# A four-layer trunk on one core: first MLP block by token tiles, hi and lo planes regrouped, adaLN loads respread

## The chip, the core and the metric

The kernel runs on one core of a Trainium2 chip, as one program. The metric is device time in microseconds (us) of one execution. The engines named below are TensorE (PE in the rows, its weight loads PEld), VectorE (DVE), ScalarE (ACT), GpSimd (POOL) and SyncE (SP), whose instruction queue issues nearly all loads from memory.

## What is computed

256 tokens of width 1024 pass four layers. Each layer has a token mixer (MLA attention in layers 0 and 3, a gated convolution in layer 1, a pooling mixer in layer 2) and then an MLP. In outline, with `mod` the adaLN vector of the layer:

```python
c_act = silu(c)
for i in range(4):
    mod = c_act @ ada_w[i] + ada_b[i]           # 1024 x 6144
    sh_m, sc_m, gt_m, sh_f, sc_f, gt_f = split(mod, 6)
    h = rmsnorm(x, g[i, 0]) * (1 + sc_m) + sh_m
    y = mixer_i(h)
    x = x + gt_m * rmsnorm(y, g[i, 1])
    h = rmsnorm(x, g[i, 2]) * (1 + sc_f) + sh_f
    y = square(relu(h @ w1[i])) @ w2[i]         # 1024 -> 4096 -> 1024
    x = x + gt_f * rmsnorm(y, g[i, 3])
```

## The kernel before

Tokens lie in two tiles of 128. Every fp32 operand of the large products is split into a `hi` part of type fp32r and a `lo` rest, and a product is the sum of three matmuls: hi by hi, lo by hi, hi by lo. A weight tile of 512 KB arrives as `raw`; ScalarE casts it to `hi` (`load`, L173), VectorE subtracts to get `lo` (L174). There are 5 buffers for `raw` and 6 each for `hi` and `lo`.

**The MLP** (`ffn`) has 16 blocks of 256 hidden columns, c = 0 to 15. For a block, TensorE runs `colhalf` twice (L587, L589: the w1 part, into a bank h), ScalarE and VectorE make relu, square, and its parts gh and gl (L632 to L637), and TensorE runs `rowblock` (L561, L564, L565: the w2 part). The w2 part of a block is run behind the w1 part of the next, so that the relu chain lies beside it. The last two blocks share one `rowblock`, which goes through the four result banks y00, y01, y10, y11 one after the other.

**adaLN.** The product with `ada_w` is cut into units of 1 MB (`araw`, four buffers), eight units to a group (shift and scale of the mixer, of the MLP, or both gates). A unit is either multiplied on TensorE (`ada_mm`) or added up on VectorE (L222, `acc`, two instructions a unit); a group that has an `acc` ends with a flush on TensorE. The tables `MIX` and `FF` say how many units go into each block or stage, how many go to TensorE at the boundary, and how many loads are issued ahead at block 14 (`CF`): `ada_fetch(ahead)`.

**The boundary** between two stages (here: the head of a stage) is a chain. Squares of y, the gate row `bc_g`, the residual into xs, squares of xs, the scale `dg` (L371), transposes of tile 0 (L377), the same for tile 1 (L388, L395), and then the first block of the next stage. `bc_g` and `bc_a` are rows that GpSimd writes to memory (`rowd`) and reads back to all partitions.

**Order.** A list scheduler sets the order on PE, DVE, ACT and POOL; in heads `line()` fixes it in the order of the code. SP's queue has the order in which loads are written in the code. Each engine takes its instructions in its order, and an issue on SP waits until the buffer that it fills is free.

## Time and profile before

| what | value |
|---|---|
| median of three runs | 1191.03 us (1190.92 to 1191.21) |
| the profiled execution | 1190.78 us, span 1189.0 us |
| TensorE busy | 1137.4 us, 96% |
| VectorE busy | 848.2 us, 71% |
| ScalarE busy | 647.1 us, 54% |
| mean granted clock of TensorE | 0.982 of full speed |

The span is the time from the first to the last instruction on the core; the rest of the execution's 1190.78 us lies around it. Busy time counts matmuls, vector and scalar instructions, not waits and not the issue of transfers. A start in a timeline is counted from the beginning of the span.

### The profile page before, as it was taken

How to read it: one execution, taken by the hardware profiler on the slowest of the kernel's cores; microseconds unless marked ns; L12 is line 12 of the kernel's file. 1: busy time of each engine (PE TensorE's matmuls, PEld its weight loads, DVE VectorE, ACT ScalarE, POOL GpSimd, SP SyncE). 2: the span in 40 equal slices, each digit the busy share in tenths (PEclk: the TensorE clock that was granted, in tenths of full speed). 3: DMA queues.
4: the chain of work that ended last, by engine and by line, in shares of the span. 5: the costliest groups of instructions: out<-in, count | busy, mean ns of one | idle time of the engine just before them, and what ended most of it. 6: DMA issues, size and time to landing. Idle time of an engine off the chain costs nothing.

```text
span 1189.0 us, 17562 instructions
## 1 busy us (share of the span) xinstructions
PE 1137.4 (96%) x6654; PEld 917.5 (77%) x6654; DVE 848.2 (71%) x1205; ACT 647.1 (54%) x1144; POOL 52.9 (4%) x120
## 2 busy tenths in 40 slices
PE   7899989999999999999999989999998999999997
PEld 4667768888868867778788768787867877888886
DVE  3699688777665666868887777787776996655554
ACT  3364575556653244655565465455555665656553
POOL 1000010000010010000000210000011001000000
PEclk9999989999999999999999989999998999999999
DMA  9768758588726784878887567789625432765550
GB/s 347 300 276 314 298 220 316 220 317 298 267 72 240 257 312 188 312 308 353 327 321 279 201 233 280 304 337 337 243 80 214 164 115 81 234 199 187 182 190 36
DMA packets 73384, 290.01 MB, mean 244 GB/s; under 512 B 9986, under 2 KB 15234, under 8 KB 61012
## 3 DMA queue, kind: packets, MB, share of 16 engines
q1 hardware_dynamic: 70484, 280.44, 64.4%
q0 software_dynamic: 2816, 8.46, 2.0%
q8 instruction: 52, 0.85, 0.3%
q14 instruction: 32, 0.26, 0.1%
HBM read 286.57 MB, written 2.29 MB: 243 GB/s over the span
## 4 chain that ended last, share of the span: by engine, by line
PE 55%; DVE 5%; ACT 3%; DMA 3%; issue 3%; POOL 2%; SPq 0%; DVEq 0%; POOLq 0%; ACTq 0%
PE h L587 14%; PE y L561 7%; PE h L589 7%; PE y L564 7%; PE y L565 7%; PE dw_ps L986 2%; ACT junk L135 1%; DMA raw<-in_w_dram 1%; PE pw L561 1%; PE adap L256 1%; PE pw L565 1%; PE pw L564 1%; POOL r L121 1%; DVE acc L222 1%; DVE lo L174 1%
## 5 line engine op out<-in xcount | busy, mean ns | idle before, releaser
L174 DVE TENSOR_TENSOR lo<-raw,hi 128x1024 fp32r<-128x1024 f32 (+1 forms) x336 | 395.5, 1195 | 133.9 <-ACT hi L173 132.8
L173 ACT CAST hi<-raw 128x1024 fp32r<-128x1024 f32 (+1 forms) x336 | 339.8, 1029 | 98.6 <-PE h L587 37.6
L587 PE MATMUL h<-hT,hi 128*128 128x512 f32 x1024 | 367.1, 401 | 0.0
L589 PE MATMUL h<-hT,lo 128*128 128x256 f32 x1024 | 288.8, 283 | 0.0
L587 PEld LDWEIGHTS h<-hT,hi 128*128 128x128 f32 x1024 | 193.9, 190 | 46.2
L589 PEld LDWEIGHTS h<-hT,lo 128*128 128x128 f32 x1024 | 194.9, 190 | 10.9 <-issue 8.4
L561 PE MATMUL y<-hi,gh 128*128 128x512 f32 x512 | 200.6, 392 | 0.0
L564 PE MATMUL y<-lo,gh 128*128 128x512 f32 x512 | 200.0, 391 | 0.0
L565 PE MATMUL y<-hi,gl 128*128 128x512 f32 x512 | 199.1, 390 | 0.0
L632 ACT COPY r<-h 128x256 f32<-128x256 f32 x128 | 47.6, 372 | 156.4 <-PE h L589 156.2
L222 DVE SCALAR_TENSOR_TENSOR acc<-araw,c_act,acc 128x1024 f32<-128x1024 f32 x98 | 120.6, 1280 | 0.1
L561 PEld LDWEIGHTS y<-hi,gh 128*128 128x128 f32 x512 | 96.1, 188 | 24.4 <-issue 2.5
L565 PEld LDWEIGHTS y<-hi,gl 128*128 128x128 f32 x512 | 96.1, 188 | 20.8 <-DVE gl L637 0.4
L564 PEld LDWEIGHTS y<-lo,gh 128*128 128x128 f32 x512 | 96.2, 188 | 18.5 <-issue 0.8
L633 DVE TENSOR_TENSOR r<-h,r 128x256 f32<-128x256 f32 x128 | 53.6, 421 | 45.8 <-ACT r L632 45.4
L634 ACT ACTIVATE r<-r 128x512 f32<-128x512 f32 x64 | 40.4, 631 | 45.6 <-DVE r L633 45.6
L637 DVE TENSOR_TENSOR gl<-r,gh 128x512 fp32r<-128x512 f32 x64 | 44.2, 690 | 23.4 <-ACT gh L636 23.3
L500 DVE TENSOR_TENSOR v<-y,bc_g 128x512 f32<-128x512 f32 x32 | 21.8, 688 | 33.6 <-ACT junk L135 22.7
L561 PE MATMUL y<-hi,hT 128*128 128x512 f32 (+1 forms) x112 | 42.2, 384 | 0.0
L564 PE MATMUL y<-lo,hT 128*128 128x512 f32 (+1 forms) x112 | 42.1, 378 | 0.0
L565 PE MATMUL y<-hi,hT 128*128 128x512 f32 (+1 forms) x112 | 41.9, 377 | 0.0
L635 ACT ACTIVATE r<-r 128x512 f32<-128x512 f32 x64 | 40.3, 629 | 1.0
(243 smaller groups left out, 1438.1 us busy)
## 6 DMA issues: line engine op xcount, KB each, us to landing
raw<-in_w_dram SPq DMA_DIRECT2D x256, 512.0 KB
araw<-in_ada_w_dram SPq DMA_DIRECT2D x96, 1024.0 KB
raw<-in_w_pw_dram SPq DMA_DIRECT2D x24, 512.0 KB
raw<-in_w_o_dram SPq DMA_DIRECT2D x16, 512.0 KB
u<-ud SPq DMA_DIRECT2D x32, 132.0 KB
raw<-in_w_ukv_dram SPq DMA_DIRECT2D x8, 512.0 KB
bc_g<-rowd POOLq DMA_DIRECT2D x8, 512.0 KB, 4.3
bc_a<-rowd POOLq DMA_DIRECT2D x7, 512.0 KB, 4.0
```

What stands on the lines that cost most here:

```text
L173: put(A.copy(h, raw), "act")
L174: put(V.tensor_tensor(l, raw, h.bitcast(F32), op=ALU.subtract), "dve")
L222: V.scalar_tensor_tensor(acc, raw[:, sl], ck, acc, op0=ALU.mult, op1=ALU.add)
L561: mm = T.matmul(o, ah, bh, start=start, stop=False, skip_group_check=True)
L564: T.matmul(o, ah, bl, start=False, stop=False, skip_group_check=True)
L565: return T.matmul(o, al, bh, start=False, stop=stop, skip_group_check=True)
L587: T.matmul(b, wh[:, s], pair[:, kk].rearrange("p a t -> p (a t)"), start=(kk == 0), stop=False, skip_group_check=True)
L589: T.matmul(b[:, 0:S], wl[:, s], pair[:, kk, 0], start=False, stop=(kk == KT - 1), skip_group_check=True)
L632: A.copy(rf, hb[:, S:])
L633: V.tensor_tensor(rf, hb[:, 0:S], rf, op=ALU.add)
L634: A.activation(r, r, AF.Relu)
L637: gli = V.tensor_tensor(gl, r, gh.bitcast(F32), op=ALU.subtract)
```

## The change

Five things change. (1) Behind each head but the first and those of the pool and the last MLA, the first block (block 0 of the MLPs, the first of the convolution) is computed by `headblock` in three pieces: the hi plane of tile 0 with hi and lo weights, before tile 1 is transposed (32 matmuls of 128 columns); half of the lo plane of tile 0 between the transposes of tile 1 (8); and the rest behind them (40 of 128 columns and 8 of 256). Its result is ready for relu without the copy and the addition. (2) `colhalf` and `colblock` run all matmuls of the hi weights first, those of `lo` (the rest plane) last, and the planes of h are stored as hi plane, then lo plane. (3) The tables are respread: nearly every MLP block now has one unit or two, the boundaries one, and blocks 13 to 15 of FFN1 have two each with three loads ahead at block 14. 17 units are left to TensorE, 28 before; flushes are 13, 11 before. (4) `gate_row` sends the gate row as soon as its group is done. (5) In a head both copies of tile 0's planes on ScalarE stand ahead of the squares of tile 1.

```diff
@@ -180,7 +180,8 @@
-    todo = [(i, g, k) for i in range(DEPTH) for g in (0, 2, 1) for k in range(KT)][KT:]
+    todo = [(i, g, k) for i in range(DEPTH) for g in ((0, 2, 1) if i else (0, 1, 2))
+            for k in range(KT)][KT:]
     nfetched = [0]
     units = []
     scope = [None]
@@ -316,6 +317,14 @@
         bct[tag] = t
+    sent = set()
+
+    def gate_row(i):
+        if (i, 1) in rows and i not in sent:
+            sent.add(i)
+            bcast("g", rows[(i, 1)], 0)
+
+
     def prep(row):
         bcast("a", row, 1)
         bct["sh"] = row
...
     def planes():
-        t = act.tile([P, KT, 2, S], F32R, tag="hT", name="hT")
+        t = act.tile([P, 2, KT, S], F32R, tag="hT", name="hT")
         both[0] = t
-        return [t[:, :, 0], t[:, :, 1]]
+        return [t[:, 0], t[:, 1]]
...
@@ -535,27 +544,27 @@
                 residual(1, [v], r1)
                 nc.sync.dma_start(out[1, :, v[0]], xs[:, 1, v[0]])
             return
-        residual(1, v1, r1)
         def fill0(h):
             o = (slice(None), slice(4 * h, 4 * h + 4), slice(0, P))
             line("act", A.copy(planes[0][o], bs[h]))
-            line("dve", V.tensor_tensor(planes[1][o], bs[h], planes[0][o].bitcast(F32),
-                                        op=ALU.subtract))
+            return lambda: line("dve", V.tensor_tensor(
+                planes[1][o], bs[h], planes[0][o].bitcast(F32), op=ALU.subtract))
         if tokens is None:
-            fill0(0)
+            low = [fill0(h) for h in range(2)]
+            if first is not None:
+                first(0)
+        residual(1, v1, r1)
         ms = squares(1)
+        if tokens is None:
+            low[0]()
         r = rsqrt_eps(*cols(ms), eng=V)
         if tokens is not None:
             tokens(scaled(1), r)
         else:
-            rest = transposed1(r, *planes)
-            next(rest)
-            fill0(1)
-            for _ in rest:
-                pass
+            transposed1(r, *planes, first, low[1])
         gate["pool"] = gate["pow"]
-        gate["free"] = GFREE
+        gate["free"] = GFREE if first is None else 0
     def mm3(o, ah, al, bh, bl, start, stop, behind=None):
         mm = T.matmul(o, ah, bh, start=start, stop=False, skip_group_check=True)
@@ -565,28 +574,72 @@
         return T.matmul(o, al, bh, start=False, stop=stop, skip_group_check=True)
+
     def colblock(src, hh, hl, name):
         parts = [load(src[p]) for p in range(2)]
         b = bank("h", name)
-        for p, (wh, wl) in enumerate(parts):
-            for k in range(4):
-                kk = 4 * p + k
-                for f in range(2):
-                    s = slice(k * 256 + f * P, k * 256 + f * P + P)
-                    mm3(b[:, 256 * f:256 * f + 256], wh[:, s], wl[:, s], hh[:, kk], hl[:, kk],
-                        start=(kk == 0 and f == 0), stop=(kk == KT - 1))
+        def w(p, kk, f):
+            s = (kk % 4) * 256 + f * P
+            return parts[kk // 4][p][:, s:s + P]
+        for kk in range(KT):
+            for f in range(2):
+                bf = b[:, S * f:S * f + S]
+                T.matmul(bf, w(0, kk, f), hh[:, kk], start=(kk == 0 and f == 0), stop=False,
+                         skip_group_check=True)
+                T.matmul(bf, w(1, kk, f), hh[:, kk], start=False, stop=False,
+                         skip_group_check=True)
+        for kk in range(KT):
+            for f in range(2):
+                T.matmul(b[:, S * f:S * f + S], w(0, kk, f), hl[:, kk], start=False,
+                         stop=(kk == KT - 1), skip_group_check=True)
         return b
+
+
+
+    def headblock(src, hh, hl):
+        parts = [load(src[p]) for p in range(2)]
+        bs = []
+
+        def mm(p, pl, kk, c0, w, stop=False):
+            b = bs[0]
+            for f in range(2):
+                s = (kk % 4) * 256 + f * P
+                for q in p:
+                    line("pe", T.matmul(b[:, S * f + c0:S * f + c0 + w],
+                                        parts[kk // 4][q][:, s:s + P], pl[:, kk, c0:c0 + w],
+                                        start=(pl is hh and kk == 0 and f == 0 and q == 0 and c0 == 0),
+                                        stop=stop, skip_group_check=True))
+
+        def stage(n):
+            if n == 0:
+                bs.append(bank("h", "h0"))
+                for kk in range(KT):
+                    mm((0, 1), hh, kk, 0, P)
+            elif n == 1:
+                for kk in range(4):
+                    mm((0,), hl, kk, 0, P)
+            else:
+                for kk in range(KT):
+                    mm((0, 1), hh, kk, P, P)
+                for kk in range(4):
+                    mm((0,), hl, kk, P, P)
+                for kk in range(4, KT):
+                    mm((0,), hl, kk, 0, S, kk == KT - 1)
+            return bs[0]
+        return stage
     def colhalf(parts, pair, f, name):
         b = bank("h", name)
+        def w(p, kk):
+            s = (kk % 4) * 256 + f * P
+            return parts[kk // 4][p][:, s:s + P]
         for kk in range(KT):
-            wh, wl = parts[kk // 4]
-            s = slice((kk % 4) * 256 + f * P, (kk % 4) * 256 + f * P + P)
-            T.matmul(b, wh[:, s], pair[:, kk].rearrange("p a t -> p (a t)"), start=(kk == 0),
-                     stop=False, skip_group_check=True)
-            T.matmul(b[:, 0:S], wl[:, s], pair[:, kk, 0], start=False, stop=(kk == KT - 1),
+            T.matmul(b, w(0, kk), pair[:, :, kk], start=(kk == 0), stop=False,
+                     skip_group_check=True)
+        for kk in range(KT):
+            T.matmul(b[:, 0:S], w(1, kk), pair[:, 0, kk], start=False, stop=(kk == KT - 1),
                      skip_group_check=True)
         return b
@@ -622,16 +675,21 @@
             scope[0] = fp
             pend = []
             for c in range(NFC):
-                parts = [load(w1[i, c][p]) for p in range(2)]
+                if c:
+                    parts = [load(w1[i, c][p]) for p in range(2)]
                 r = fp.tile([P, 512], F32, tag="r", name="r", bufs=2)
                 gh = fp.tile([P, 512], F32R, tag="gh", name="gh")
                 gl = fp.tile([P, 512], F32R, tag="gl", name="gl")
-                for f in range(2):
-                    hb = colhalf(parts, pair, f, "h1")
-                    rf = r[:, S * f:S * f + S]
-                    A.copy(rf, hb[:, S:])
-                    V.tensor_tensor(rf, hb[:, 0:S], rf, op=ALU.add)
-                A.activation(r, r, AF.Relu)
+                if c == 0:
+                    hb = first(2)
+                    A.activation(r, hb, AF.Relu)
+                else:
+                    for f in range(2):
+                        hb = colhalf(parts, pair, f, "h1")
+                        rf = r[:, S * f:S * f + S]
+                        A.copy(rf, hb[:, S:])
+                        V.tensor_tensor(rf, hb[:, 0:S], rf, op=ALU.add)
+                    A.activation(r, r, AF.Relu)
                 A.activation(r, r, AF.Square)
                 A.copy(gh, r)
                 gli = V.tensor_tensor(gl, r, gh.bitcast(F32), op=ALU.subtract)
...
@@ -1127,14 +1186,12 @@
                                                    op0=ALU.mult, op1=ALU.add))
             hs.append(xa)
         head(tokens=tokens)
-        for k in range(2):
-            fetch(w1[i, 0, k])
         ada(units)
+        gate_row(i)
         wp = [load(pool_w[j, k], gains) for k in range(2)]
         bh, bl = load(pool_b[j], gain_row)
         prep(rows[(i, 2)])
         shift_rows()
-        bcast("g", rows[(i, 1)], 0)
         ph, pl = planes()
         for t in range(NT):
             for h in range(2):
@@ -1173,15 +1230,15 @@
     MIX = {
         0: ([2, 4, 2, 3, 3, 2], 0, 1),
-        1: ([0, 0, 2, 0, 1, 2, 1, 0, 1], 3, 4),
-        2: (1, 3, 3),
-        3: ([0, 2, 0, 0, 0, 0], 0, 0),
+        1: ([0, 0, 2, 0, 1, 2, 1, 1, 1], 1, 3),
+        2: (1, 1, 3),
+        3: ([0, 0, 0, 0, 0, 0], 0, 0),
     }
     FF = {
-        0: ([1, 2, 1, 0, 2, 0, 3, 0, 2, 2, 0, 0, 0, 1, 0, 0], 1, 3),
-        1: ([1, 1, 0, 1, 2, 2, 1, 2, 2, 2, 1, 0, 0, 1, 0, 0], 4, 3),
-        2: ([0, 2, 0, 2, 0, 3, 1, 1, 2, 0, 2, 0, 1, 3, 0, 1], 3, 0),
-        3: ([0, 0, 0, 0, 0, 0, 0, 0, 0, 0, 0, 0, 0, 0, 0, 0], 0, 0),
+        0: ([1, 1, 2, 1, 1, 1, 1, 1, 1, 1, 1, 1, 1, 1, 1, 0], 1, 3),
+        1: ([1, 1, 1, 1, 1, 1, 1, 2, 1, 1, 2, 1, 1, 2, 2, 2], 1, 3),
+        2: ([1, 1, 1, 1, 1, 1, 2, 1, 1, 2, 1, 1, 2, 1, 2, 2], 1, 2),
+        3: ([0] * NFC, 0, 0),
     }
     qgs = cp.tile([P, q_g.shape[0], 3], F32, name="qgs")
     kgs = cp.tile([P, kv_g.shape[0], 2], F32, name="kgs")
```

**SyncE's queue, end of FFN1.** Before, the issues between the w1 tiles of block 14 (`raw_6077`) and the w2 tiles of block 13 (`raw_6135`, `raw_6141`); `araw` are adaLN units, `bg` a bias row:

```order
L155 DMA raw_6077<-in_w1_dram 128x1024
L196 DMA araw_6128<-in_ada_w_dram 128x2048
L199 DMA bg_91<-in_ada_bg_dram 4x1024
L196 DMA araw_6131<-in_ada_w_dram 128x2048
L196 DMA araw_6133<-in_ada_w_dram 128x2048
L155 DMA raw_6135<-in_w2_dram 128x1024
L155 DMA raw_6141<-in_w2_dram 128x1024
```

The same place in the changed kernel, from w1 of block 14 (`raw_6215`) to w2 of block 13 (`raw_6281`, `raw_6287`):

```order
L155 DMA raw_6215<-in_w1_dram 128x1024
L197 DMA araw_6266<-in_ada_w_dram 128x2048
L197 DMA araw_6270<-in_ada_w_dram 128x2048
L200 DMA bg_91<-in_ada_bg_dram 4x1024
L197 DMA araw_6275<-in_ada_w_dram 128x2048
L197 DMA araw_6277<-in_ada_w_dram 128x2048
L197 DMA araw_6279<-in_ada_w_dram 128x2048
L155 DMA raw_6281<-in_w2_dram 128x1024
L155 DMA raw_6287<-in_w2_dram 128x1024
```

Five units instead of three now stand between them, and there are four buffers for units.

**VectorE, end of FFN1.** Before, from the w2 tiles of block 12 (`lo_6038`) to the first w2 tile of block 13 (`lo_6138`); `r_5986` and `gl_5988` are block 13's relu chain:

```order
L174 TENSOR_TENSOR lo_6038<-raw_6035,hi_6037 128x1024
L633 TENSOR_TENSOR r_5881<-h1_5903,r_5881 128x256
L174 TENSOR_TENSOR lo_6044<-raw_6041,hi_6043 128x1024
L174 TENSOR_TENSOR lo_6074<-raw_6071,hi_6073 128x1024
L637 TENSOR_TENSOR gl_5883<-r_5881,gh_5882 128x512
L174 TENSOR_TENSOR lo_6080<-raw_6077,hi_6079 128x1024
L633 TENSOR_TENSOR r_5986<-h1_5989,r_5986 128x256
L633 TENSOR_TENSOR r_5986<-h1_6008,r_5986 128x256
L637 TENSOR_TENSOR gl_5988<-r_5986,gh_5987 128x512
L222 SCALAR_TENSOR_TENSOR acc_5539<-araw_6031,c_act_112,acc_5539 128x1024 x2
L174 TENSOR_TENSOR lo_6138<-raw_6135,hi_6137 128x1024
```

The changed kernel, from block 13's gl (`gl_6122`) on; `r_6221` and `gl_6223` are block 14's relu chain, `lo_6284` and `lo_6290` the w2 tiles of block 13:

```order
L695 TENSOR_TENSOR gl_6122<-r_6120,gh_6121 128x512
L223 SCALAR_TENSOR_TENSOR acc_5960<-araw_6165,c_act_112,acc_5960 128x1024 x2
L223 SCALAR_TENSOR_TENSOR acc_5960<-araw_6169,c_act_112,acc_5960 128x1024 x2
L691 TENSOR_TENSOR r_6221<-h1_6224,r_6221 128x256
L691 TENSOR_TENSOR r_6221<-h1_6243,r_6221 128x256
L695 TENSOR_TENSOR gl_6223<-r_6221,gh_6222 128x512
L223 SCALAR_TENSOR_TENSOR acc_5960<-araw_6266,c_act_112,acc_5960 128x1024 x2
L223 SCALAR_TENSOR_TENSOR acc_5960<-araw_6270,c_act_112,acc_5960 128x1024 x2
L174 TENSOR_TENSOR lo_6284<-raw_6281,hi_6283 128x1024
L174 TENSOR_TENSOR lo_6290<-raw_6287,hi_6289 128x1024
```

The w2 tiles of block 13 stood ahead of block 14's relu chain; now they stand behind it, and behind two more units.

**TensorE, head of FFN3.** Before, the transposes of tile 0 (x4, the second half) and of tile 1, after which block 0 begins with 512 columns at a time:

```order
L377 MATMUL hT_ps_9437<-dg_9429,xa_9420 128x128 x4
L395 MATMUL hT_ps_9468<-ident_93,xa_9466 128x128
L395 MATMUL hT_ps_9470<-ident_93,xa_9466 128x128
L395 MATMUL hT_ps_9473<-ident_93,xa_9466 128x128 x2
L395 MATMUL hT_ps_9477<-ident_93,xa_9466 128x128 x4
```

The changed kernel at the same place; h0 is block 0's bank, and the two h0 rows repeat to 32 matmuls where a line is left out:

```order
L387 MATMUL hT_ps_9630<-dg_9622,xa_9613 128x128 x4
L608 MATMUL h0_9648<-hT_9579,hi_9582 128x128
L608 MATMUL h0_9648<-hT_9579,lo_9583 128x128
...
L406 MATMUL hT_ps_9695<-ident_93,xa_9693 128x128
L406 MATMUL hT_ps_9697<-ident_93,xa_9693 128x128
L406 MATMUL hT_ps_9700<-ident_93,xa_9693 128x128 x2
L608 MATMUL h0_9648<-hT_9579,hi_9582 128x128 x8
L406 MATMUL hT_ps_9712<-ident_93,xa_9693 128x128 x4
```

The transposes of tile 1 now stand behind 32 matmuls of block 0, and 8 more stand between them.

## Rows read from the trace of the kernel before

**Rows 1.** The page, parts 1 and 2: PE's busy time; granted clock in 40 slices.

```profile
PE 1137.4 (96%) x6654; PEld 917.5 (77%) x6654; DVE 848.2 (71%) x1205; ACT 647.1 (54%) x1144; POOL 52.9 (4%) x120
PEclk9999989999999999999999989999998999999999
```

**Rows 2.** Two windows: us; busy us of PE, PEld, DVE, ACT, POOL; clock, DMA share, GB/s.

```profile
499.00:519.00 20.00, 20.00 (x102) 16.95 (x101) 13.04 (x16) 11.37 (x17) 0.00 (x0) 1.00 1.00 398
691.00:700.00 9.00, 5.75 (x25) 4.92 (x25) 6.33 (x14) 5.00 (x15) 2.94 (x6) 0.52 0.48 183
```

**Rows 3.** Timeline of TensorE inside FFN1: start, length, engine, line.

```profile
647.88 0.40 PE L587 MATMUL h<-hT,hi 128*128 128x512 f32 x1
648.94 0.40 PE L587 MATMUL h<-hT,hi 128*128 128x512 f32 x1
```

**Rows 4.** Timeline of TensorE in the pool: matmuls of 256 columns in a run.

```profile
677.20 0.28 PE L564 MATMUL y<-lo,hT 128*128 128x256 f32 x1
677.90 0.28 PE L564 MATMUL y<-lo,hT 128*128 128x256 f32 x1
```

**Rows 5.** The page, part 5: groups with busy us, mean ns of one, idle before.

```profile
L174 DVE TENSOR_TENSOR lo<-raw,hi 128x1024 fp32r<-128x1024 f32 (+1 forms) x336 | 395.5, 1195 | 133.9 <-ACT hi L173 132.8
L173 ACT CAST hi<-raw 128x1024 fp32r<-128x1024 f32 (+1 forms) x336 | 339.8, 1029 | 98.6 <-PE h L587 37.6
L632 ACT COPY r<-h 128x256 f32<-128x256 f32 x128 | 47.6, 372 | 156.4 <-PE h L589 156.2
L222 DVE SCALAR_TENSOR_TENSOR acc<-araw,c_act,acc 128x1024 f32<-128x1024 f32 x98 | 120.6, 1280 | 0.1
```

**Rows 6.** Timeline, VectorE and ScalarE, from FFN2's block 13 to the next head.

```profile
857.07 7.26 DVE L222 SCALAR_TENSOR_TENSOR acc<-araw,c_act,acc 128x1024 f32<-128x1024 f32 x6
874.95 0.42 DVE L633 TENSOR_TENSOR r<-h,r 128x256 f32<-128x256 f32 x1
877.38 0.69 DVE L637 TENSOR_TENSOR gl<-r,gh 128x512 fp32r<-128x512 f32 x1 [2.01 <-ACT gh L636]
877.99 2.48 DVE L222 SCALAR_TENSOR_TENSOR acc<-araw,c_act,acc 128x1024 f32<-128x1024 f32 x2
880.38 0.68 DVE L500 TENSOR_TENSOR v<-y,bc_g 128x512 f32<-128x512 f32 x1
888.18 0.40 ACT L371 ACTIVATE dg<-ident,r 128x128 f32<-128x128 f32 x1 [0.42 <-POOL r L121]
```

**Rows 7.** The page, part 6: transfers, KB each, us from issue to landing.

```profile
araw<-in_ada_w_dram SPq DMA_DIRECT2D x96, 1024.0 KB
bc_g<-rowd POOLq DMA_DIRECT2D x8, 512.0 KB, 4.3
```

**Rows 8.** Timeline of SyncE's queue at the end of the convolution.

```profile
429.16 12.88 SPq L196 DMA_DIRECT2D araw<-in_ada_w_dram  x5
442.13 2.02 SPq L155 DMA_DIRECT2D raw<-in_w_pw_dram  x4
```

**Rows 9.** Timeline of ScalarE at the same place.

```profile
451.90 1.05 ACT L173 CAST hi<-raw 128x1024 fp32r<-128x1024 f32 x1 [1.24 <-DMA raw<-in_w_pw_dram]
```

**Rows 10.** Timeline, VectorE's waits for the gate row; TensorE at the first.

```profile
148.93 1.29 DVE L500 TENSOR_TENSOR v<-y,bc_g 128x512 f32<-128x512 f32 x2 [7.58 <-DMA bc_g<-rowd]
149.81 1.06 PE L256 MATMUL adap<-araw,c_act 128*32 128x512 f32 x8
687.40 1.29 DVE L500 TENSOR_TENSOR v<-y,bc_g 128x512 f32<-128x512 f32 x2 [3.30 <-DMA bc_g<-rowd]
```

**Rows 11.** Timeline of TensorE: 128-column passes in FFN1's and FFN3's head.

```profile
472.97 2.05 PE L377 MATMUL hT_ps<-dg,xa 128*128 128x128 f32 x16
1002.27 2.18 PE L395 MATMUL hT_ps<-ident,xa 128*128 128x128 f32 x8 [2.55 <-DVE xa L388]
```

**Rows 12.** Timeline of TensorE: half a flush in FFN2; a unit in the last MLA.

```profile
744.12 1.05 PE L256 MATMUL adap<-acc,ones_c 128*32 128x512 f32 x4
918.31 1.06 PE L256 MATMUL adap<-araw,c_act 128*32 128x512 f32 x8
```

More of the change, by code (lines that the diff above doesn't have):

```diff
@@ L363, in shifts @@
         b = bank(tag, "hT_ps")
-        T.matmul(b, bct["shT"], pick[:, 4 * h:4 * h + 4].unsqueeze(2).to_broadcast([40, 4, P]),
-                 start=True, stop=False, skip_group_check=True)
+        line("pe", T.matmul(b, bct["shT"],
+                            pick[:, 4 * h:4 * h + 4].unsqueeze(2).to_broadcast([40, 4, P]),
+                            start=True, stop=False, skip_group_check=True))
         return b
@@ L376, in transposed0, with transposed1 @@
                 kk = 4 * h + k
-                T.matmul(b[:, k * P:(k + 1) * P], xa[:, kk * P:(kk + 1) * P], dg,
-                         start=False, stop=True, skip_group_check=True)
+                line("pe", T.matmul(b[:, k * P:(k + 1) * P], xa[:, kk * P:(kk + 1) * P], dg,
+                                    start=False, stop=True, skip_group_check=True))
             bs.append(b.rearrange("p (k t) -> p k t", k=4))
         return bs
-    def transposed1(r, hi, lo):
+    def transposed1(r, hi, lo, first, low0):
         xa = tmp.tile([P, D], F32, tag="xa", name="xa")
@@ L386, in transposed1 @@
         for ks in ((0, 1), (2, 3), (4, 5, 6, 7)):
+            if ks[0] == 4 and first is not None:
+                first(1)
             sl = slice(ks[0] * P, (ks[-1] + 1) * P)
@@ L392, in transposed1 @@
                     b = bank("y", "hT_ps")
[L393 removed]
                 bk = b[:, (k % 4) * P:(k % 4 + 1) * P]
[L395 to L404 removed]
+                gate["pe"] = line("pe", T.transpose(bk, xa[:, k * P:(k + 1) * P], ident))
+                bks.append((bk, (slice(None), k, slice(P, S)), bct["shc"][:, k:k + 1]))
+        for bk, o, sh in bks:
+            gate["act"] = line("act", A.activation(hi[o], bk, AF.Identity, bias=sh))
+        low0()
+        for bk, o, sh in bks:
+            gate["dve"] = line("dve", V.scalar_tensor_tensor(
+                lo[o], bk, sh, hi[o].bitcast(F32), op0=ALU.add, op1=ALU.subtract))
     def planes():
[L407 removed]
+        t = act.tile([P, 2, KT, S], F32R, tag="hT", name="hT")
         both[0] = t
[L409 removed]
+        return [t[:, 0], t[:, 1]]
     both = [None]
@@ L506, in residual, with boundary @@
                                                op0=ALU.mult, op1=ALU.add))
-    def boundary(ys, units, planes=None, tokens=None):
+    def boundary(ys, units, planes=None, tokens=None, first=None):
         ada(units)
@@ L613, in y_banks, with ffn @@
         return [[bank("y", f"y{t}{n}") for n in range(2)] for t in range(NT)]
-    def ffn(i, h, units, ahead, mid):
+    def ffn(i, h, units, ahead, mid, first):
         hh, hl = h
@@ L963, in mla, with conv @@
         return y
-    def conv(i, h, units, ahead):
+    def conv(i, h, units, ahead, first):
         j = i // 3
@@ L1009, in conv @@
             pend, dgs, uds = [], [], []
-            for m in range(2):
-                for p in range(2):
-                    fetch(w_pw1[j, m, p])
+            for p in range(2):
+                fetch(w_pw1[j, 1, p])
             for m in range(KT):
@@ L1016, in conv @@
                         fetch(w_pw1[j, m + 2, p])
-                hb = colblock(w_pw1[j, m], hh, hl, "pw1")
+                hb = colblock(w_pw1[j, m], hh, hl, "pw1") if m else first(2)
                 sg = vp.tile([P, S], F32, tag="sg", name="sg", bufs=2)
@@ L1043, in conv @@
             shift_rows()
-            bcast("g", rows[(i, 1)], 0)
             sh_, sl_ = planes()
@@ L1136, in pool @@
         shift_rows()
-        bcast("g", rows[(i, 1)], 0)
         ph, pl = planes()
@@ L1206, in tile_trunk @@
             hi, lo = planes()
+            first = None
+            if m or i % 3 == 1:
+                first = headblock(w1[i, 0] if m else w_pw1[i // 3, 0], hi, lo)
             if s == 0:
@@ L1210, in tile_trunk @@
             else:
-                head(planes=(hi, lo))
+                head(planes=(hi, lo), first=first)
             if m:
@@ L1224, in mid @@
                         consts = pool_consts(pool_p, (i + 1) // 3)
-                y = ffn(i, (hi, lo), sched[0], sched[2], mid)
+                y = ffn(i, (hi, lo), sched[0], sched[2], mid, first)
             else:
-                y = (mla if i % 3 == 0 else conv)(i, (hi, lo), sched[0], sched[2])
+                args = (i, (hi, lo), sched[0], sched[2])
+                y = mla(*args) if i % 3 == 0 else conv(*args, first)
 def layout(inp):
```

15 lines of the change are left out of this document (4 added, 11 removed).

## The prediction, made before the changed kernel was run

> **What bounds the kernel now.** I read the busy times and the clock line first, then windows of the MLPs, then the timeline at each place that the change touches, and the waits last. TensorE is busy for 1137.4 us of the 1189.0 us span [rows 1]. Inside the MLPs it never waits: of a 20 us window in FFN1 it works all 20.00 us, while VectorE works 13.04 [rows 2]. Time is lost only in the heads: the nine microseconds around FFN2's head hold 5.75 us of TensorE work, at a granted clock of 0.52 (the lower of the two levels, 1.2 GHz, for nearly all of it) [rows 2]. So the MLPs can be made shorter by fewer or shorter matmuls alone, they get longer as soon as a weight tile is late, and a head gets shorter only if its chain does. The profiled execution took 1190.78 us, 0.25 us less than the median of the runs; I sum against it and add that at the end.
>
> **1. The w1 part in another order.** Now a matmul of 512 columns and one of 256 alternate; three such pairs take 648.94 - 647.88 = 1.06 us, 0.353 us a pair [rows 3]. Matmuls of 256 columns in a run start (677.90 - 677.20) / 6 = 0.117 us apart, six steps lying between the two rows [rows 4]. If 512 columns in a run then cost twice that, 0.234 us at most, a pair costs 0.351 us; I take 0.347, since a run saves the change of shape. 16 pairs a block save 0.09 us, and 60 blocks 5 us. Bounds: nothing, and 5.6 us. **-5.**
>
> **2. The first block by token tiles.** A 128-column fp32r matmul isn't in the trace. The nearest rows are f32 transposes of 128 columns: 16 passes in 2.05 us, so 0.12 us a pass once the last one's own length is taken off [rows 11]. At that price the first piece, 32 x 0.12 = 3.8 us, lies in the 2.55 us that TensorE idles ahead of tile 1's transposes [rows 11] and in the microsecond by which tile 1 now comes later (term 5), and 48 matmuls, 5.8 us, stand behind tile 1, where 16 pairs, 5.65 us, stood before. That is a gain of nothing: the same time, and half the matmuls have only been made smaller. Bounds from rows: 0.06 us each (half of 256 columns [rows 4]) gives 48 x 0.06 = 2.9 us less in each of five heads, -14; 0.234 us each (as if 512 columns) gives 48 x 0.114 = 5.5 us more behind tile 1, and 3.7 us more of the first piece of which the wait hides none, 9 us a head, +45. I take 0.12, as the row is nearest in shape and in what bounds it. **0.** The Trainium skill (TensorE: Matmul & The Clock Gate, Back-to-back issue gap) gives about 81 ns per matmul in a sustained stream of 128 columns with a weight load each; by it the term would be 48 x 0.039 x 5 = 9 us gained. No row here shows that for fp32r.
>
> **3. The gate row early.** In FFN0's head VectorE waits 7.58 us for `bc_g`, until 148.93; TensorE is through with y only shortly before 149.81 [rows 10]. With the row sent a group earlier, TensorE's end is late next, so 7.58 can't be gained; I take 2.7, bounds 0 and 4. In the pool the 3.30 us wait for `bc_g` ahead of FFN2 [rows 10] stays, as its two transfers stay behind the chain of tile 1 on GpSimd. **-2.7.**
>
> **4. Convolution.** Ahead of the w_pw2 tiles SyncE issues five units and needs 12.88 us for it, waiting for buffers; the tiles issued from 442.13 on reach ScalarE at 451.90, 9.8 us later [rows 8, 9]. Four units stand there now: one fifth of that, some 2 us, and FFN1's head follows with fewer units on TensorE. I take 4 us for both, bounds 0 and 6. The added flushes, in FFN0 and in the convolution, cost two halves of 1.05 us each [rows 12]: 2.1 us in FFN0, where TensorE is the bound, and half of it in the convolution, which waits at its end; +3.3 with their starts. **-0.7.**
>
> **5. The last MLA.** Two units go, 1.06 us each on TensorE [rows 12], and with them two row operations on VectorE: -2.5. But in its head the units of FFN2's block 15 are two instead of one: now 2.48 us of `acc` lie between gl and the first v [rows 6], then 4.9, and two operations on the row (0.7 us each, as v) stand between the two v. With the two copies ahead of the squares the scale of tile 1 is another microsecond late: +4.1. **+1.6.** The same order at the end of FFN1, where no `acc` stood, costs the pool's chain some 2.3 us and a flush inside the last `rowblock` 1 us. **+3.3.**
>
> **6. The ends of the MLPs.** Here I see the largest term, and it is a wait. Take block 14 of FFN1. When TensorE is through with its w1 part, it wants the w2 tiles of block 13. In the changed order SyncE issues these behind five units, and the fifth, with four buffers, must wait until the first has been added up. That stands on VectorE behind block 14's own gl. So, from the end of the w1 part: copy 0.37, then from the addition to the end of gl 874.95 to 878.07, 3.1 us [rows 5, 6]; two `acc`, 2.48 us [rows 6]; then the last unit (1 MB) and the first w2 tile (0.5 MB) have to come. A 0.5 MB row takes 4.3 us from issue to landing [rows 7], the tiles behind five units took 9.8 [rows 8, 9]; with 1.5 MB I take 5.5. Then hi, 1.03, and lo, 1.2 [rows 5]: 0.4 + 3.1 + 2.5 + 5.5 + 1.0 + 1.2 = 13.7 us, less one matmul that needs hi alone. TensorE has nothing else to do. **+13.5**, bounds 9.6 (only the four `acc`, 4.9 us, and one lo count, and the tile is there) and 17.8 (landing as in rows 8 and 9). What speaks against it: six `acc` in a row, 7.26 us, stand on VectorE in FFN2 now [rows 6] and TensorE doesn't wait. But there the w2 tiles of that block have been split ahead of them.
>
> At FFN0's and FFN2's block 14 the second w2 tile of block 13 is cast behind parts of block 14's relu chain: copy, hi and lo, 2.6 us, less a matmul or two, **+1.9**; with addition and relu ahead of it **+3**. After a stall of 13 us I expect TensorE on its lower clock level for a few us, as in the head in rows 2: **+2**, bounds 0 and 4.
>
> The sum is -5 + 0 - 2.7 - 0.7 + 1.6 + 3.3 + 13.5 + 1.9 + 3 + 2 = +16.9, so 1190.8 + 16.9 = 1207.7; with 0.25 for the median, 1208 us, 1.4% slower.
>
> **The rivals.**
>
> *The ends don't stall* (faster). If the w2 tiles of block 13 land before TensorE is through with block 14's w1 part, in all three MLPs, terms 13.5, 1.9, 3 and 2 go, and the sum is -3.5: 1187.5 us. For it speaks that VectorE has 7 us free of 20 [rows 2] and that six `acc` hurt nothing. It decides at one point: whether the fifth unit's issue is held by an `acc` that follows block 14's gl. If that buffer comes free a block earlier, this is the case. The order speaks against it. Chance 0.12.
>
> *Cheap small matmuls* (still slower). At 0.06 us per 128 columns term 2 is -14, and 1194 us come out. For it: 256 columns take 0.117 us, so columns and not weight loads set the pace there [rows 4]. Against it: transposes of 128 columns are no faster than that [rows 11]. Chance 0.18.
>
> *Dear small matmuls* (much slower). If a 128-column fp32r matmul takes as long as one of 512, term 2 is +30 to +45: 1238 to 1253 us. For it: not one fp32r matmul of the kernel before has fewer than 256 columns, so no row excludes it. Against it: f32 passes of 128 columns run at 0.12. Chance 0.17.
>
> The sum above with its own bounds, 1198 to 1215, has 0.53.
>
> **How the numbers follow.** I predict the likeliest case, 1207 us. Its own range with the bounds of terms 6 is 1198 to 1215. The range for 8 in 10 takes in the cheap small matmuls below and the start of the dear ones above: 1188 to 1240. Cases outside are most of the dear one and half of the case without stalls. A measurement of this kernel can tell about 0.2%, 2.4 us, from no change. Faster: the case without stalls and a little of the cheap matmuls, 0.13. Same: between these, 0.08. Slower: 0.79.
>
> **What would show it.** In the changed profile, a gap of TensorE of 10 to 18 us behind the w1 part of FFN1's block 14, released by hi or lo of a w2 tile, with SyncE waiting on `acc` ahead of it; gaps of 2 to 3 us at the same place in FFN0 and FFN2; whole blocks elsewhere about 0.1 us shorter; in the heads, starts of the 128-column matmuls 0.12 us apart; no wait for `bc_g` in FFN0's head. The prediction is wrong if the gap at FFN1's block 14 is under 5 us, if the 128-column matmuls start 0.06 or over 0.2 us apart, or if the regrouped w1 part is slower than the alternating one, as its moving operand now comes from two places 2048 elements apart.

## The result and the profile after

The changed kernel takes 1241.74 us (median of 4 runs, 1228.28 to 1245.29) against 1190.97 of the kernel before on the same chip: ratio 1.0395, 95% interval 1.0351 to 1.0439 (a little under the quotient of these two medians, 1.0426). It is slower, as forecast, but by 47 us by the ratio, 51 between the medians, and not by 17, and the time lies just outside the range. The profiled execution took 1245.29 us, its span 1243.5; it is the longest of the four. The versions below ran on three chips, each beside the kernel before on its own chip, so they are compared by their ratios; differences in us between versions are rougher. One execution of the version with 256 columns below took 2265.52 us and is left out of its median and ratio.

The page of the changed kernel, beside [rows 1]: TensorE is busy 37.4 us longer, VectorE 21.4, and the line of the granted clock is lower.

```profile
PE 1174.8 (94%) x6846; PEld 966.7 (78%) x6846; DVE 869.6 (70%) x1219; ACT 646.1 (52%) x1136; POOL 54.6 (4%) x120
...
PEclk9899999999979989999997868999997999999999
```

Much of that is no added work: it ran at a lower clock. The mean granted clock is 0.954 (0.982 before). The stretches at the lower level (1.2 GHz), added up over the span, are 114.6 us; before they were 43.6.

Windows of the changed kernel, busy time (and instructions) of PE, PEld, DVE, ACT, POOL, then granted clock, DMA share, GB/s; the first is the convolution's first block, then the end of FFN1, the pool, FFN2's first block and the block behind it, as [rows 2] showed for before:

```profile
354.00:371.00 17.00, 16.85 (x80) 16.74 (x81) 11.52 (x22) 7.92 (x14) 0.00 (x0) 0.50 0.06 14
...
657.00:672.00 15.00, 3.77 (x9) 2.59 (x10) 9.21 (x9) 4.93 (x6) 0.00 (x0) 0.54 0.68 267
705.00:722.00 17.00, 12.97 (x55) 12.06 (x56) 9.55 (x13) 3.75 (x6) 3.64 (x5) 0.52 0.61 208
729.00:753.00 24.00, 24.00 (x114) 23.34 (x113) 12.79 (x23) 9.90 (x21) 2.23 (x4) 0.51 0.30 112
753.00:773.00 20.00, 20.00 (x103) 17.10 (x103) 15.18 (x18) 13.62 (x21) 0.00 (x0) 0.99 0.90 328
```

The row to look at is 729 to 753: TensorE waits for nothing, is busy all 24.00 us, and has half its clock for nearly all of it. The clock comes back at 753.4, behind the last eight matmuls of the block, which have 256 columns, and the first of 512 columns of the next block.

TensorE's timeline of the changed kernel (start, length, engine, line, what it writes and reads, and in brackets the idle time before it and what ended it): first the 128-column matmuls of FFN0's first block and those of FFN2's, then the first matmul of the w2 part behind block 14 in FFN0, FFN1 and FFN2, and the bias matmul of the pool.

```profile
153.88 0.31 PE L608 MATMUL h<-hT,hi 128*128 128x128 f32 x1
154.03 0.28 PE L608 MATMUL h<-hT,lo 128*128 128x128 f32 x1
154.14 0.28 PE L608 MATMUL h<-hT,hi 128*128 128x128 f32 x1
...
732.33 0.45 PE L608 MATMUL h<-hT,hi 128*128 128x128 f32 x1
732.59 0.41 PE L608 MATMUL h<-hT,lo 128*128 128x128 f32 x1
732.80 0.41 PE L608 MATMUL h<-hT,hi 128*128 128x128 f32 x1
...
321.40 1.20 PE L570 MATMUL y<-hi,gh 128*128 128x512 f32 x4 [1.41 <-ACT hi L173]
...
668.19 1.22 PE L570 MATMUL y<-hi,gh 128*128 128x512 f32 x2 [13.26 <-ACT hi L173]
...
910.47 2.07 PE L570 MATMUL y<-hi,gh 128*128 128x512 f32 x4 [2.52 <-ACT hi L173]
...
709.03 0.79 PE L1219 MATMUL y<-lo,ones_r 1*128 1x512 f32 x1 [6.18 <-DVE lo L174]
```

The waits at the ends of the MLPs are where they were forecast and about as long; the 6.18 us in the pool were not forecast. The 128-column matmuls start 0.11 us apart in FFN0, as forecast, and 0.21 us apart in FFN2.

Where the 54.5 us between the two spans arose, from the starts of the w1 parts of blocks 2 and 15 of each MLP; the second column adds up the prediction's terms for that stretch, with the w1 order at 1.25 us an MLP:

| stretch | predicted | measured |
|---|---|---|
| up to FFN0's block 2 | -2.7 | -2.3 (178.3 to 176.0) |
| FFN0, blocks 2 to 15 | +2.8 | +3.6 |
| convolution and FFN1's head | -2.8 | +13.1 |
| FFN1, blocks 2 to 15 | +14.3 | +13.6 |
| pool and FFN2's head | +3.3 | +18.8 |
| FFN2, blocks 2 to 15 | +1.7 | +3.3 |
| last MLA and FFN3's head | +1.6 | +5.5 |
| FFN3, blocks 2 to 15, and the rest | -1.2 | -1.1 |

Inside the MLPs the sum was right to 2 us; nearly all that is missing, some 35 us, is in the stages between them.

### The profile page after: what moved, and what is told of

Read it like the earlier page. It is cut to its first block, busy times and chain, and to the rows that moved or that the text cites. A ratio compares the mean times of both kernels' runs of the same rounds, so it can differ in the third digit from the quotient of the medians.

```text
span 1243.5 us, 17959 instructions
## 1 busy us (share of the span) xinstructions
PE 1174.8 (94%) x6846; PEld 966.7 (78%) x6846; DVE 869.6 (70%) x1219; ACT 646.1 (52%) x1136; POOL 54.6 (4%) x120
## 4 chain that ended last, share of the span: by engine, by line
PE 86%; DVE 4%; ACT 3%; issue 3%; DMA 2%; POOL 1%; SPq 1%; POOLq 0%; DVEq 0%; ACTq 0%
PE h L639 18%; PE y L570 11%; PE y L574 11%; PE y L573 11%; PE h L642 9%; PE h L608 5%; PE adap L257 3%; PE s_ps L957 2%; PE dw_ps L1046 1%; PE pw L587 1%; PE pw L589 1%; PE pw L593 1%; POOL r L121 1%; PE hT_ps L387 1%; PE hT_ps L406 1%
## 5 line engine op out<-in xcount | busy, mean ns | idle before, releaser
L173 ACT CAST hi<-raw 128x1024 fp32r<-128x1024 f32 (+1 forms) x336 | 336.4, 1028 | 138.1 <-PE y L574 72.7
L639 PE MATMUL h<-hT,hi 128*128 128x512 f32 x960 | 239.6, 392 | 0.0
L639 PEld LDWEIGHTS h<-hT,hi 128*128 128x128 f32 x960 | 176.3, 189 | 37.2 <-issue 3.4
L223 DVE SCALAR_TENSOR_TENSOR acc<-araw,c_act,acc 128x1024 f32<-128x1024 f32 x116 | 143.0, 1279 | 0.0
L642 PEld LDWEIGHTS h<-hT,lo 128*128 128x128 f32 x960 | 131.0, 190 | 11.8 <-issue 2.5
L642 PE MATMUL h<-hT,lo 128*128 128x256 f32 x960 | 134.5, 283 | 0.0
L608 PE MATMUL h<-hT,hi 128*128 128x128 f32 (+1 forms) x280 | 66.3, 327 | 0.0
L692 ACT ACTIVATE r<-r 128x512 f32<-128x512 f32 x60 | 37.9, 632 | 42.6 <-DVE r L691 42.6
L608 PEld LDWEIGHTS h<-hT,hi 128*128 128x128 f32 x280 | 56.9, 240 | 0.0
L608 PE MATMUL h<-hT,lo 128*128 128x128 f32 x160 | 45.3, 317 | 0.0
L570 PE MATMUL y<-hi,hT 128*128 128x512 f32 (+1 forms) x112 | 44.5, 399 | 0.0
```

Source lines behind the costliest of these rows:

```text
L173: put(A.copy(h, raw), "act")
L223: V.scalar_tensor_tensor(acc, raw[:, sl], ck, acc, op0=ALU.mult, op1=ALU.add)
L570: mm = T.matmul(o, ah, bh, start=start, stop=False, skip_group_check=True)
L608: line("pe", T.matmul(b[:, S * f + c0:S * f + c0 + w], parts[kk // 4][q][:, s:s + P], pl[:, kk, c0:c0 + w], start=(pl is hh and kk == 0 an ...
L639: T.matmul(b, w(0, kk), pair[:, :, kk], start=(kk == 0), stop=False, skip_group_check=True)
L642: T.matmul(b[:, 0:S], w(1, kk), pair[:, 0, kk], start=False, stop=(kk == KT - 1), skip_group_check=True)
```

## The experiments

Theory A: in a head, a wait lets the clock fall, and the narrow matmuls that follow don't bring it back, so that they run at half speed for as long as they last. Rival B: these 35 us are new waits that the tables make (loads and buffers), and the clock only shows them. Rival C: the pieces of 128 columns are dear at any clock.

**One piece of 256 columns.** The changed kernel, but the first block in one piece behind tile 1.

```diff
-            if n == 0:
+            if n == 2:
                 bs.append(bank("h", "h0"))
                 for kk in range(KT):
-                    mm((0, 1), hh, kk, 0, P)
...
+                    mm((0, 1), hh, kk, 0, S)
                 for kk in range(KT):
...
                     mm((0,), hl, kk, 0, S, kk == KT - 1)
...
```

> The changed kernel with one edit: headblock computes the first block in one piece behind tile 1, with 48 matmuls of 256 columns in place of 88 in three pieces, of which 80 have 128 columns; everything else, the tables too, as in the changed kernel. Theory A (narrow matmuls that begin at the lower clock level keep TensorE there): the long stretches at the lower level behind the convolution's head (17.1 us) and FFN2's head (23.9 us) shrink to some 3.4 to 7 us, the first blocks there end some 6 to 9 us earlier, and the time falls by 12 to 17 us to about 1226 us; in FFN0, FFN1 and FFN3, where the narrow matmuls ran at 112 ns, nothing is lost or up to 1 us a head. Theory B (the lower level follows from the longer waits, whatever the columns): both stretches stay, and the time stays within 4 us of 1242.

Measured: 1233.95 us (median of three), ratio 1.0357 (1.0300 to 1.0414), 7.8 us under the changed kernel by the medians, 0.4% by the ratios. Neither theory's time came out, and the two intervals overlap, so the times alone show no gain. What happens to the clock is seen in the trace. TensorE's timeline of this kernel, FFN2's first block:

```profile
729.24 2.14 PE L406 MATMUL hT_ps<-ident,xa 128*128 128x128 f32 x8 [3.54 <-DVE xa L400]
731.03 0.56 PE L608 MATMUL h<-hT,hi 128*128 128x256 f32 x1
731.39 0.41 PE L608 MATMUL h<-hT,lo 128*128 128x256 f32 x1
731.60 0.41 PE L608 MATMUL h<-hT,hi 128*128 128x256 f32 x1
...
734.16 0.35 PE L608 MATMUL h<-hT,hi 128*128 128x256 f32 x1
734.36 0.28 PE L608 MATMUL h<-hT,lo 128*128 128x256 f32 x1
734.47 0.28 PE L608 MATMUL h<-hT,hi 128*128 128x256 f32 x1
```

At the lower level matmuls of 256 columns also start 0.21 us apart, so 128 columns cost about what 256 cost, at both levels. But here the clock is back at 734.2, 3.1 us into the block, while the narrow stream stayed low to its end. The kernel before shows the same in the convolution's head, where its first block has 256 columns. The clock fell at 353.5, behind the wait in this row of that kernel, and was back at 356.9, within the block:

```profile
351.65 0.83 PE L395 MATMUL hT_ps<-ident,xa 128*128 128x128 f32 x4 [1.57 <-DVE xa L388]
```

By the profiled executions the stretch of the convolution and FFN1's head is 7.2 us shorter than in the changed kernel, that of the pool and FFN2's head 8.4. In the other heads little is gained with 48 matmuls in place of 88: nothing fills the wait ahead of tile 1's transposes any more, 3.4 to 4.7 us in every head, and the clock now falls in FFN0's, FFN1's and FFN3's heads too (3.4 to 6.8 us each).

**TensorE kept busy.** The changed kernel, with 12 matmuls of 256 columns ahead of tile 0's transposes in FFN2's head and 5 ahead of tile 1's in the convolution's. Their results are overwritten; they are no part of the computation.

```diff
+    WARM = {(2, 1): (12, 0), (1, 0): (0, 5)}
...
+            line("pe", T.matmul(b[:, 0:S], ident, c_act.rearrange("p k a -> p (k a)"),
+                                start=True, stop=True, skip_group_check=True))
```

> The changed kernel with 17 added matmuls of 256 columns whose results are overwritten: 12 in FFN2's head ahead of tile 0's transposes and 5 in the convolution's head ahead of tile 1's, both where TensorE waits; nothing else is touched. Theory A (the narrow matmuls of a first block keep the clock level at which they begin): FFN2's head begins at the upper level, its 128-column matmuls start 0.112 us apart in place of 0.213, its first block ends some 9 us earlier, and the convolution's no longer falls either; 9 to 17 us less, 1225 to 1233 us. Theory B (in FFN2 narrow matmuls are slow for another reason, or the added work only delays): they stay 0.213 us apart, and the time stays at 1242 or above.

Measured: 1232.30 us, ratio 1.0338 (1.0316 to 1.0359), 9.4 us less by the medians and 0.6% by the ratios, by adding work. The two intervals still overlap a little; the last experiment repeats the step with the intervals apart. TensorE's timeline of this kernel in FFN2's head (the trace counts each of the 12 fp32 matmuls as two passes; one record is missing):

```profile
722.73 5.12 PE L386 MATMUL hT_ps<-c_act,ident 128*128 128x256 f32 x23
...
730.60 0.31 PE L620 MATMUL h<-hT,hi 128*128 128x128 f32 x1
730.75 0.27 PE L620 MATMUL h<-hT,lo 128*128 128x128 f32 x1
730.86 0.28 PE L620 MATMUL h<-hT,hi 128*128 128x128 f32 x1
```

From the first to the last of this block's 88 matmuls, tile 1's transposes among them, it is now 11.3 us instead of 20.7. This is theory A, shown in the trace by its removal, and C isn't the cause of what is missing: the price is 0.11 us at the upper level in all five heads, as the sum had it.

**FFN1's units earlier.** The changed kernel, with one row of a table.

```diff
-        1: ([1, 1, 1, 1, 1, 1, 1, 2, 1, 1, 2, 1, 1, 2, 2, 2], 1, 3),
+        1: ([1, 2, 1, 2, 2, 2, 1, 2, 2, 2, 2, 1, 1, 0, 0, 0], 1, 3),
```

> The changed kernel with FFN1's 21 units moved forward: none in blocks 13 to 15, two in most earlier blocks; the three loads ahead at block 14 stay. The prediction's term 6: the 13.3 us wait of TensorE behind block 14's w1 part goes, and a stretch at the lower clock level with it, so 13 to 16 us less, about 1227 us. If the wait in the pool (6.2 us) and the late gate row behind it come from the units added up behind FFN1's last gl as well, these go too and FFN2's head begins warm: 25 to 32 us less, about 1213 us. Rival (SyncE's queue isn't what holds the tiles): the wait stays or moves to another block, and the time stays within 5 us.

Measured: 1224.41 us, ratio 1.0268 (1.0221 to 1.0316), 17.3 us less. The wait of 13.26 us is 2.52, and the pool's 6.18 is gone too. By the profiled executions FFN1's blocks 2 to 15 are 6.6 us shorter, pool and FFN2's head 11.7: less than the wait comes back in FFN1, where the moved units now stand in earlier blocks. FFN2's head still ran low for 27.3 us, behind a wait of 4.26. In the convolution's head the same wait of 1.1 us as in the changed kernel did not drop the clock this time: whether a short wait does so varies, and with it the spread of the runs.

**The tables of before.** The changed kernel with both tables and the order of layer 0's groups as before.

> The changed kernel with the tables of before (units per block and stage, order of the groups of layer 0); tiles, order of the w1 part, early gate row and the copies in the heads as changed. If the tables make the waits of TensorE (1.4, 13.3, 6.2, 2.5 and the two of 5.0 and 3.4 us in the last MLA's head), these go, about 32 us together with the clock behind them, and what is left is the narrow matmuls at the lower level in one or two heads, 7 to 9 us each, against 5 us from the w1 part: 1187 to 1203 us. If the tables cost only the FFN1 wait: about 1226 us.

Measured: 1207.99 us, ratio 1.0138 (1.0061 to 1.0214), a little above the forecast. No wait of a microsecond is left at the ends of the MLPs or in the pool, so the tables, with the order of the groups, are worth 2.6%, 31 us. What is left is in the main one head: up to FFN0's block 2 the profiled execution is 12.1 us longer than before. Windows of this kernel around FFN0's head, columns as above:

```profile
150.00:156.00 6.00, 2.44 (x18) 1.18 (x13) 4.82 (x9) 3.11 (x9) 1.19 (x3) 1.00 0.43 178
156.00:180.00 24.00, 24.00 (x109) 23.37 (x109) 12.74 (x22) 10.60 (x21) 1.98 (x4) 0.50 0.35 132
```

The same picture at another place: a wait of 3.56 us ahead of tile 0's transposes, then 24 us of narrow work at half the clock.

**The w1 order alone.** The kernel before, with the regrouped `colhalf` and `colblock` and the planes that belong to them.

> The kernel before with only colhalf, colblock and the layout of the planes as changed. The prediction's term 1: 0.09 us less in each of some 70 blocks, 5 to 6 us less, 1185 to 1186 us. Rival (the moving operand in two places costs as much as the change of shape did): within 1 us of before.

Measured: 1184.16 us, ratio 0.9942 (0.9919 to 0.9964): 7 us gained.

**Everything but tiles and tables.** The changed kernel with the tables of before and no `headblock`: w1 order, early gate row, layer 0's new order, and both copies ahead of the squares.

```diff
-            if m or i % 3 == 1:
+            if False:
                 first = headblock(w1[i, 0] if m else w_pw1[i // 3, 0], hi, lo)
```

> The changed kernel with the tables of before and without headblock (first blocks as the other blocks, pool loads w1 early as before); w1 order, early gate row and the copies in the heads stay. Theory A: the stretch of 23.9 us at the lower level in FFN0's head that the kernel with old tables and tiles showed goes; 1184 to 1190 us, as the w1 order alone (1184). If the tiles don't cost that: within 4 us of 1208.

Measured: 1194.36 us, ratio 1.0006 (0.9985 to 1.0027). The forecast missed: against the w1 order alone some part of it costs 0.6%, 8 us by the ratios.

**Tiles on old tables, kept busy.** The version just above, but with `headblock`, and overwritten matmuls in six heads.

> The changed kernel with the tables of before, tiles as changed, and added matmuls of 256 columns (results overwritten) where TensorE waits in seven heads: 3 to 6 ahead of tile 1's transposes, 8 ahead of tile 0's in FFN2. Theory A: no first block runs at the lower level except in FFN0, where the wait ahead of tile 0 (3.6 us) has none ahead of it; if that head falls, 1195 to 1200 us, if it stays up, 1180 to 1186. Theory B: no gain against the same kernel without the added matmuls (1208).

Measured: 1195.24 us, ratio 1.0031 (1.0016 to 1.0046), with 13.5 us at the lower level in all, none of it in FFN0's head. For that case 1180 to 1186 was forecast, which missed. Even with the clock up, the tiles bring nothing that can be measured against the version without them (1.0006).

**The w1 order, kept busy.** The w1 order alone and 4 to 13 overwritten matmuls in six heads.

> The kernel before with the w1 order (1184 us) and added matmuls of 256 columns (results overwritten) where TensorE waits in six heads, 4 to 8 in a place. If a wait of 2 to 4 us is what drops the clock, the 37 us at the lower level become less than 20, and 4 to 9 us are saved: 1175 to 1180 us. If the added matmuls delay the chains by as much as the clock gives back: 1183 to 1187.

Measured: 1182.64 us, ratio 0.9907 (0.9875 to 0.9939). The intervals overlap with those of the w1 order alone (0.9942), so a gain isn't shown. The profiled execution, with a clock of 0.997 and 6.8 us at the lower level, is the fastest of the four, 1176.08 us; the other three lie at 1182.6.

**Early gate row without the order of the copies.** The version without tiles and with old tables, but with the heads' order of before.

```diff
-            low = [fill0(h) for h in range(2)]
-            if first is not None:
-                first(0)
-        residual(1, v1, r1)
+            fill0(0)
         ms = squares(1)
...
-            transposed1(r, *planes, first, low[1])
+            rest = transposed1(r, *planes)
+            next(rest)
+            fill0(1)
```

> The kernel before with the w1 order, the gate row early and the new order of groups in layer 0, without the changed order of the copies in the heads and without the token tiles. If the order of the copies is what makes the version without tiles some 10 us slower than the w1 order alone (1194 against 1184), this one is at 1180 to 1185, and TensorE's gaps ahead of the transposes of tile 1 are 1.5 to 3.2 us as before. If the early gate row or the order of groups costs it, this one is at 1190 to 1195.

Measured: 1181.56 us, ratio 0.9899 (0.9880 to 0.9918), the lowest of all versions, though not told apart from the w1 order kept busy. Against 1.0006 this is the price of the copies' order (with the order of TensorE that the heads fix along with it): 1.07%, 12.7 us. The waits of TensorE ahead of tile 1's transposes, all heads together, first in the version with the copies ahead, then in this one; the view adds the waits of the matmuls and those of their weight loads, which lie side by side:

```profile
  DVE xa L400: 45.0, 20
```

```profile
  DVE xa L397: 28.8, 23
```

The matmuls' own share is 20.9 us with the copies ahead (3.45 us in each of six heads) and 14.4 in this version, 6.5 us less: that is half of the price, and where the rest lies isn't shown. Against the w1 order alone (0.9942) the early gate row with layer 0's order brings 0.4%, 5 us, at the edge of the two intervals.

**The same, kept busy.**

> The same with 256-column matmuls whose results are overwritten in the waits of six heads (they are no part of the computation). If the early gate row is worth its 2 to 3 us of the first MLP's head also here, 1178 to 1181; if not, 1182.6, as the w1 order with the same matmuls, or more. If the order of groups in layer 0 costs 10 us, 1190.

Measured: 1187.07 us, ratio 0.9938 (0.9915 to 0.9962): no faster than without, rather slower, as the two intervals just touch. In the first MLP's head it is 18.9 us from dg to the first relu, 15.8 without, though FFN0's block 2 still starts 2.2 us earlier than without. The loss lies in the convolution, whose stretch is 7.7 us longer: two waits of 1.50 and 1.24 us there were followed by 17.1 us at the lower level, on mixed work: matmuls of 512 columns in short runs between narrow ones. That the added matmuls cause these two waits isn't shown.

**FFN1's units earlier and TensorE kept busy.**

> The changed kernel with the units of the second MLP in its earlier blocks and with the overwritten matmuls in the heads of the third MLP and of the convolution. If the wait at the end of the second MLP and the lower clock in the heads are separate costs, their gains add: 1241.7 - 17.3 - 9.4 = 1215. If the units' place already decides the clock in these heads, 1224.

Measured: 1209.22 us, ratio 1.0129 (1.0104 to 1.0155): 32 us less than the changed kernel, where the two alone gave 17.3 and 9.4. The costs are separate, and their gains add to at least their sum. Against FFN1's units alone (1.0268) the overwritten matmuls gain 1.4%, some 15 us, with the intervals well apart: this shows theory A in the times too. Window of this kernel, FFN2's first block:

```profile
703.00:716.00 13.00, 12.95 (x109) 12.50 (x110) 9.37 (x19) 9.56 (x20) 1.68 (x3) 1.00 0.25 87
```

## Why the prediction was right in sign and short by 35 us

**Where it was right.** Term 6, with its mechanism: SyncE's queue holds the w2 tiles behind a unit that has no buffer. The timeline of the changed kernel at the end of FFN1, from the w1 part's end to the first w2 matmul:

```profile
654.97 0.37 ACT L690 COPY r<-h 128x256 f32<-128x256 f32 x1 [2.42 <-PE h L642]
657.80 0.69 DVE L695 TENSOR_TENSOR gl<-r,gh 128x512 fp32r<-128x512 f32 x1 [2.01 <-ACT gh L694]
658.41 4.87 DVE L223 SCALAR_TENSOR_TENSOR acc<-araw,c_act,acc 128x1024 f32<-128x1024 f32 x4
649.90 11.34 SPq L197 DMA_DIRECT2D araw<-in_ada_w_dram  x3
661.34 10.87 SPq L155 DMA_DIRECT2D raw<-in_w_dram  x8
667.09 1.04 ACT L173 CAST hi<-raw 128x1024 fp32r<-128x1024 f32 x1 [9.32 <-DMA raw<-in_w_dram]
```

SyncE's third unit of this row goes out when two of the four `acc` are done, and is out at 661.2; the tile is issued at 661.34 and cast at 667.09, 5.8 us later (5.5 taken); TensorE starts at 668.19, after 13.26 us (13.5 taken). FFN0 and FFN2 waited 1.41 and 2.52 (1.9 and 3 taken). Moving FFN1's units took its wait down to 2.52, and the tables of before took all three away. Term 1, from TensorE's timeline of the changed kernel in FFN1, the starts of the two halves of a w1 part:

```profile
649.21 1.98 PE L639 MATMUL h<-hT,hi 128*128 128x512 f32 x8
...
651.98 2.00 PE L639 MATMUL h<-hT,hi 128*128 128x512 f32 x8
```

Half a w1 part now takes 651.98 - 649.21 = 2.77 us, so a pair takes 0.346 us (0.347 taken), a block 0.08 us less from start to start, and the kernel with this alone 7 us less (5 taken). Term 3: VectorE's wait for `bc_g` in FFN0's head is gone, and FFN0's block 2 starts 2.3 us earlier (2.7 taken).

**The step that failed: term 2, through the clock.** Its price, 0.12 us for 128 columns, is right at the upper level: 0.112 in FFN0, FFN1 and FFN3. The Trainium skill (TensorE: Matmul & The Clock Gate, Back-to-back issue gap) gives about 81 ns for 128 columns. The trace doesn't agree: 112 ns here, nearly the 120 ns of 256 columns. But I took the price from rows at the upper level alone, and for the lower one I booked a fixed +2 us behind the longest wait, as if every stream brought the clock back in a few microseconds, as in [rows 2]. Those rows have 512 and 256 columns. Of the new block's 88 matmuls 80 have 128, they are 11.3 us at the upper level and 20.7 at the lower. Where the clock had fallen at a wait of 1 to 5 us ahead of them it stayed low to their end: in the changed kernel in FFN2's head (1.66 us waited, 9.4 us lost) and behind the first piece in the convolution's (1.12 us waited). I had given "dear small matmuls" 0.17, on the ground that no row excluded them; 0.21 us a matmul came true in two heads of five, for another reason. *Cheap small matmuls* fell, and with them their reason that columns set the pace: 128 columns start 0.112 us apart, not 0.06.

**Terms 4 and 5, mis-sized.** The convolution was to gain and lost: from dg of its head to dg of FFN1's it took 140.0 us after, 127.3 before. From dg to the start of its second block it is 21.7 us, 15.5 before, and in its last part there is a new wait of 2.44 us for `u` and 10 us at the lower level. With TensorE kept busy in the head the same stretch is 132.1; what of the rest is the load order and what the clock stays open. In the pool TensorE waited 6.18 us for the `lo` of a bias row that VectorE split only behind tile 1's chain. I had put +3.3 on pool and FFN1's last flush; the wait went away when FFN1's units were moved, so it came from these late units. Whether by their loads or by the 4.85 us of `acc` that they put behind FFN1's last gl stays open. This wait and the 9.4 us of FFN2's first block make most of the 18.8 us of that stretch. In the last MLA's head TensorE waits 4.95 and 3.44 us, 1.07 and 3.23 before, and the stretch is 5.5 us longer where 1.6 were taken. The order of the two copies I charged once, as "another microsecond" in the last MLA's head. The scale of tile 1 waits for squares that stand behind the copies, in FFN2's head 2.61 us where it was 0.66 before. VectorE's timeline, first two rows of the changed kernel (the first is FFN0's gate row, no longer waited for), then one of the kernel before:

```profile
149.68 0.69 DVE L509 TENSOR_TENSOR v<-y,bc_g 128x512 f32<-128x512 f32 x1 [0.32 <-ACT junk L135]
...
734.72 0.21 DVE L117 TENSOR_SCALAR v<-ms 128x1 f32<-128x1 f32 x1 [2.61 <-ACT junk L135]
...
696.62 0.21 DVE L117 TENSOR_SCALAR v<-ms 128x1 f32<-128x1 f32 x1 [0.66 <-ACT junk L135]
```

The wait behind it is 3.45 us in every head where no tiles lie in it, and the copies' order costs 12.7 us there in all. The first piece of the tiles fills it, but in the same step the tiles double the block, from 5.6 us to 9.9 (80 x 0.112 + 8 x 0.12): what goes into the wait is only what was added. So tiles and copies together are no faster than the copies alone (1.0031 with the clock up, 1.0006), and both are 1% slower than the w1 order and the gate row by themselves.

**The rivals.** The ends did stall, so the faster case fell. Of the three theories, A holds for the heads and B for the ends of the MLPs and the pool; C fell as a cause, though a matmul of 128 columns costs about as much as one of 256. From the best version to the changed kernel, by ratios: 0.9899, with the copies' order 1.0006, with tiles and new tables 1.0395 (with tiles, the old tables and layer 0's old order 1.0138). In us of 1191 these steps are -12, +13 and +46. The prediction's terms for them were -8 (terms 1 and 3), about +1, and +24. So the w1 order and the gate row (with layer 0's order) were worth more than forecast, and the copies' order, and the tiles and tables with the clock behind their waits, were mis-sized by 12 and 22 us. Left open: why a wait of 1.1 us dropped the clock in one run and the same wait in another run did not.

## What to carry to other kernels

When work is cut into narrow matmuls behind a wait, price it at both clock levels, and ask whether the stream itself brings the clock back: here 88 narrow matmuls cost 11.3 or 20.7 us, and 17 useless 256-column ones in two heads gained some 15 us where FFN1's units stood early. Count what a queue holds in front of an urgent load in buffers, not in bytes: the fifth unit with four buffers made TensorE wait 13.26 us. Time the parts of a bundled change by themselves: two of the five parts here, with layer 0's order, were worth 1%, and the other three cost 5%.

## What the runs showed that was not expected

A matmul of 128 columns (fp32r) started 0.112 us after the one before at the upper level and 0.213 at the lower, about as much as one of 256 columns (0.120 and 0.213). A TensorE busy for 24.00 of 24.00 us, nearly all of it with them, stood at a granted clock of 0.51, and with a stream of 256 columns in the same head the clock was back at the upper level after 3.1 us.
